# Six residual tiles with buffers of their own, and another model behind the scheduler's order

## The chip, the cores and the metric

The kernel runs on one core of a Trainium2 chip. The metric is device time in microseconds (us) of one execution. A profile is one execution taken by the hardware profiler; engines are named PE (TensorE, matrix products), PEld (its weight loads), DVE (VectorE), ACT (ScalarE), POOL (GpSimd) and SP (SyncE, here the queue that issues most DMAs).

## The reference, cut to what matters

Two networks in a row on a sequence of 512 positions with 1024 channels. The first has one block that mixes by a recurrence (8 heads) and by a stick-breaking attention (8 heads), joins both, and adds the result to its input. The second has two layers: a short convolution and a neighbourhood attention, each followed by a gated feed-forward, with a context of 256 positions beside it.

```
def first_block(x, c, ...):
    mod = silu(c) @ ada_w + ada_b              # shift, scale, gate
    h = rmsnorm(x, norm_g) * (1 + scale) + shift
    p = h @ w_in
    y_rwkv = rwkv7_group(p[..., :RWKV_COLS], ...)     # recurrence over 512 steps
    y_sb   = stick_breaking_group(p[..., RWKV_COLS:], sb_g)
    y = concatenate([y_rwkv, y_sb]) @ w_out
    x = x + gate * y                           # x is the residual
    return rmsnorm(x, final_g)

def second_block(x, c, ctx, c_ctx, ...):       # two layers
    for i in range(2):
        h, hc = modulate(rms_norm(x)), modulate(rms_norm(ctx))
        y, yc = conv_mixer(h), conv_mixer(hc)  # i == 0
        y     = neighbourhood_attention(h, hc) # i == 1
        x = x + g1 * y; x = x + g2 * swiglu(modulate(rms_norm(x)))
        # the context likewise, in layer 0 alone
    return x
```

## The kernel before

All activations stand transposed, as tiles of 128 channels x 512 positions (256 for the context). A product with full accuracy is made of three fp32r matmuls (`mm3`, L172 to L174): every weight and every activation is split into a high part (a cast on ACT, L155 for weights) and a low part (a subtraction on DVE, L156). Weights come from HBM on SP's queue in tiles `st` (L167, two buffers), and their split parts `wh`, `wl` have four buffers. Products are summed in two PSUM banks called `acc`.

Block 1 (`block1`) first normalises x and makes the modulation, then runs eight generators in turn: four recurrences `rwkv_pair` (two heads each, three steps to a pair) and four attentions `sb_pair`, in the fixed succession ORDER. A recurrence computes its inputs (L903: rm, km, vm), builds chunk matrices by many small matmuls (L978 to L1018), walks through eight chunks (L1056 to L1082) and normalises the outcome (L1085 to L1101). An attention computes, for each of four query blocks and two heads, scores (L1146), two Sigmoids (L1150, L1151), a scan and a product (L1155, L1157), transposes (L1161) with a copy (L1163), and values (L1168); then it normalises (L1171 to L1179). Meanwhile POOL loads and DVE reduces the modulations of later layers (L200, L210), at low priority.

The end of block 1 is the part `tail`. It is traced behind the last attention, `sb_pair(3)`, in a memory pool of that name, which lies where the recurrences' pool `rk` was. It holds:

- the context: eight loads of `xc` (L404), squares and their sum (L254 to L263), `rstd`, and the modulated `hc` (L287 to L290);
- the products with w_out in two parts. The first part needs six of the eight results (`yh`, in the succession YORD); the second the results of recurrence 3 and attention 3 (h3, h7). For m = 0 to 5 the first part is a product in `acc` (18 matmuls), a load of the residual tile `xt` (L418, one tag, two buffers), and L420, which computes part = acc x gate + xt and so frees the bank. For m = 6, 7 the first part stays in the two `acc` banks. The second part (from L443 on) completes all eight, adds the part (L450), and sums the squares for the next norm (L453 to L460). The tiles 6 and 7 of x are loaded by L433, in another pool.

Layer 0 (`layer0`) and layer 1 (`layer1`) follow: convolution and feed-forward as long rows of products, and the neighbourhood attention (`na_pair`) with scores, softmax, transposes and values for eight pairs of heads.

What sets the order: the program is traced in one succession, which gives each instruction its priority. The framework's scheduler then plays the program on a model of the machine: an instruction whose inputs and buffers are ready in the model is handed to its engine, the one traced earliest first. The succession so found is written into each engine's queue and each DMA queue. On the chip every queue runs strictly in it, each instruction waiting on semaphores for what it needs. Pools are opened with `reuse_waits="tile"`: a tile waits only for the tiles whose memory it takes. Some edges are drawn by hand (`order`), to keep functions of one ACT table together.

Of the kernel before, what the change touches and what calls it, by code (L numbers as in the profile page):

```python
# [8 lines left out]
F32 = mybir.dt.float32  # L9
# [8 lines left out]
S = 512  # L18
SC = 256
# [65 lines left out]
class K:  # L85
# [223 lines left out]
    def block1(self):  # L309
        nc, tc, A = self.nc, self.tc, self.A  # L310
# [12 lines left out]
        with self.open(name="n1", bufs=2) as npool:  # L323
# [13 lines left out]
            rstd = npool.tile([128, S], F32, tag="nzc", name="rstd")  # L337
# [40 lines left out]
        with self.open(name="sb", bufs=1) as sb:  # L378
            with self.open(name="rk", bufs=1) as rk:
                self.rk, self.sb = rk, sb  # L380
                pl = pre[12]
                zl = rk.tile([128, S], F32, name="zl")
                self.mix(pl, self.V("mu", 12), omu[:, 12:13], zl)
                nc.scalar.activation(zl[0:64], zl[0:64], AF.Tanh)
                self.y = y
                runs = [self.rwkv_pair(p, W, h, zl, omu, oka, pre) for p in range(4)]
                for n in ORDER[:-1]:
                    if n < 4:
                        next(runs[n], None)
                    else:  # L390
                        y[n] = self.sb_pair(n - 4, W, h, sb)
            self.xp = self.pool("xp", side="right")
            self.cxp = self.pool("cxp", side="right")
            self.hcp = self.pool("hc", side="right")
            self.xas = ExitStack()
            xa = self.xas.enter_context(self.open(name="xa", bufs=1, side="right"))
            y[7] = self.sb_pair(3, W, h, sb)
            if self.dbg:
                for k in range(8):
                    nc.sync.dma_start(A['dbg_y'][k], y[k])  # L400
            with self.open(name="tail", bufs=2) as tp:
                xc = self.xc = [self.cxp.tile([128, SC], F32, tag=f"xc{k}", name=f"xc{k}") for k in range(KT)]
                for k in range(KT):
                    nc.sync.dma_start(xc[k], A["ctx"][k])  # L404
                hc = self.hc = [self.hl(self.hcp, SC, f"hc{k}") for k in range(KT)]
                gc = self.gain("gc0", "norm_mix0", mod, 8, 1)
                pc = self.psum("py")[:, :SC]
                self.sumsq(xc, SC, tp, "c", pc)
                rstd = tp.tile([128, SC], F32, name="rstd")
                since = self.rsqrt(rstd, pc, since=self.sbexp)  # L410
                self.modulate(xc, range(KT), gc, mod, 0, 1, hc, tp, "cz", rstd)
                yh, part = [], []
                for k in YORD:
                    if k == 3:
                        for m in range(6):
                            po = self.xgemm(A["w_out"][m], yh, 0, 6)
                            xt = tp.tile([128, S], F32, tag="xt", name="xt")
                            nc.sync.dma_start(xt, A["x"][m // 2, :, m % 2])  # L418
                            t = self.yp.tile([128, S], F32, tag=f"y{YORD[m]}", name="part")
                            nc.vector.scalar_tensor_tensor(t, po, self.m1[:, 16 + m, 0:1], xt,  # L420
                                                           op0=ALU.mult, op1=ALU.add)
                            part.append(t)
                        for m in (6, 7):
                            po = self.psum("acc")
                            self.gemm(po, A["w_out"][m], yh, 0, 6, last=False)
                            part.append(po)
                        w2 = self.load_w(A["w_out2"][0], 1024) + self.load_w(A["w_out2"][1], 1024)
                    t = self.hl(self.hp, S, f"h{k}")
                    self.split(t, y[k])
                    yh.append(t)  # L430
# [13 lines left out]
        for n, m in enumerate((6, 7, 0, 1, 2, 3, 4, 5)):  # L444
            po, base = (part[m], xs[m]) if m >= 6 else (self.psum("acc"), part[m])
# [828 lines left out]
```

## Time and profile before

| | us |
|---|---|
| median of 3 runs (lowest to highest) | 2109.79 (2105.21 to 2114.11) |
| the profiled execution's own time | 2113.01 |
| its span, first to last instruction | 2111.2 |
| block 1: first product of layer 0 starts at | 545.4 |
| layer 1's attention, about | 1450 to 1740 |

The profile gives busy time by engine and views of the same execution: stretches (busy time of each engine between two moments), the timeline of one engine (start, duration, line, operation, and in brackets the idle time before it with what ended it), the waits (who waited for whom), the chain of work that ended last, and all instructions that touch a tile. Ends of matmuls are modelled, so a busy PE is not PE at its peak. The granted clock is given as a share of full speed. The lines stand in the prediction, where they are used.

### The profile page before, as it was taken

To read this page: it belongs to the slowest core of one execution; us is meant where nothing else is said; L and a number is where in the kernel's file an instruction comes from. 1 tells how busy PE (TensorE), PEld (TensorE's weight loads), DVE (VectorE), ACT (ScalarE), POOL (GpSimd) and SP (SyncE) were. 2 spreads that over 40 slices of the span, in tenths; PEclk is the share of its full clock that TensorE was granted. 3 is DMA by queue.
4 is the path that set the end of the run, shared out by engine and by line. 5 is a ranking of instruction groups with operands and counts; after the bars stand their busy time and mean duration, and the time that the engine had idled before them with its cause. 6 is when DMAs were issued, how large, how long until landed. Compare 5 with 4: busy or idle time off the path is not lost.

```text
span 2111.2 us, 33545 instructions
## 1 busy us (share of the span) xinstructions
PE 2055.6 (97%) x13596; PEld 1655.4 (78%) x13596; DVE 1233.2 (58%) x2641; ACT 796.4 (38%) x1485; POOL 131.4 (6%) x212
## 2 busy tenths in 40 slices
PE   6899999998999999999999999999999999999999
PEld 3676666665788888888888888898777787888887
DVE  3868887645777756767355443354566655434443
ACT  3436444345422224221122122244777744323232
POOL 0000000000000000001001000000233200000000
PEclk9999999987999999999999999999999999999999
DMA  7432312112233321435234322222111112333333
GB/s 285 139 101 82 112 59 86 55 52 74 70 127 128 125 80 50 150 120 180 88 122 154 115 91 58 63 81 70 43 59 61 36 63 90 99 100 93 97 99 101
DMA packets 61356, 203.60 MB, mean 96 GB/s; under 512 B 6928, under 2 KB 8976, under 8 KB 61200
## 3 DMA queue, kind: packets, MB, share of 16 engines
q1 hardware_dynamic: 45360, 145.77, 21.2%
q0 software_dynamic: 15120, 55.06, 8.1%
q8 instruction: 107, 1.75, 0.3%
q10 hardware_dynamic: 720, 0.62, 0.1%
q14 instruction: 49, 0.40, 0.1%
HBM read 199.32 MB, written 2.10 MB: 95 GB/s over the span
## 4 chain that ended last, share of the span: by engine, by line
PE 87%; ACT 3%; DVE 2%; issue 1%; POOL 0%; POOLq 0%; ACTq 0%; DVEq 0%
PE acc L173 20%; PE acc L172 19%; PE acc L174 19%; PE cacc L174 5%; PE cacc L173 5%; PE cacc L172 5%; PE py L894 2%; PE pT L874 2%; PE ss L1146 1%; PE so L1168 1%; PE sm L861 1%; PE sm L862 1%; PE py L1082 1%; PE py L1080 1%; PE ss L1161 1%
## 5 line engine op out<-in xcount | busy, mean ns | idle before, releaser
L155 ACT CAST wh<-st 128x512 fp32r<-128x512 f32 (+2 forms) x481 | 292.6, 609 | 733.4 <-PE acc L173 291.8
L156 DVE TENSOR_TENSOR wl<-st,wh 128x512 fp32r<-128x512 f32 (+2 forms) x481 | 324.1, 676 | 358.3 <-ACT wh L155 354.9
L172 PE MATMUL acc<-xzzh,wh 128*128 128x512 f32 x352 | 138.7, 394 | 0.0
L174 PE MATMUL acc<-xzzh,wl 128*128 128x512 f32 x352 | 138.0, 392 | 0.0
L173 PE MATMUL acc<-xzzl,wh 128*128 128x512 f32 x352 | 138.0, 392 | 0.0
L210 DVE CUSTOM_DVE_ANT_0 junk<-ast,cb,vec 128x512 bf16<-128x512 f32 x168 | 125.2, 745 | 18.2 <-DMA ast<-in_w_ada_dram 14.6
L210 DVE CUSTOM_DVE_ANT_0 junk<-ast,cb,m 128x512 bf16<-128x512 f32 x168 | 125.4, 747 | 2.8
L200 POOL DMA_DIRECT2D ast<-in_w_ada_dram x96 | 50.9, 530 | 1026.0 <-DVE m L210 954.6
L174 PEld LDWEIGHTS acc<-xzzh,wl 128*128 128x128 f32 x352 | 66.0, 188 | 14.9
L173 PEld LDWEIGHTS acc<-xzzl,wh 128*128 128x128 f32 x352 | 66.1, 188 | 13.5 <-issue 0.5
L172 PEld LDWEIGHTS acc<-xzzh,wh 128*128 128x128 f32 x352 | 66.1, 188 | 13.4 <-issue 0.5
L172 PE MATMUL acc<-h0h,wh 128*128 128x512 f32 (+1 forms) x164 | 65.9, 402 | 3.0 <-DVE fs L642 3.0
L173 PE MATMUL cacc<-czzl,wh 128*128 128x256 f32 x240 | 68.1, 284 | 0.0
L172 PE MATMUL cacc<-czzh,wh 128*128 128x256 f32 x240 | 67.7, 282 | 0.0
L174 PE MATMUL cacc<-czzh,wl 128*128 128x256 f32 x240 | 67.2, 280 | 0.0
L174 PE MATMUL acc<-h2h,wl 128*128 128x512 f32 (+1 forms) x164 | 65.8, 401 | 0.0
L173 PE MATMUL acc<-h3l,wh 128*128 128x512 f32 (+1 forms) x164 | 65.3, 398 | 0.3 <-DVE h3l L290 0.3
L173 PE MATMUL acc<-h1l,wh 128*128 128x512 f32 (+1 forms) x164 | 65.5, 399 | 0.0
L173 PE MATMUL acc<-h6l,wh 128*128 128x512 f32 (+1 forms) x164 | 65.4, 399 | 0.1
L173 PE MATMUL acc<-h5l,wh 128*128 128x512 f32 (+1 forms) x164 | 65.2, 398 | 0.0
L174 PE MATMUL acc<-h4h,wl 128*128 128x512 f32 (+1 forms) x164 | 65.2, 398 | 0.0
L174 PE MATMUL acc<-h0h,wl 128*128 128x512 f32 (+1 forms) x164 | 65.1, 397 | 0.0
(731 smaller groups left out, 5584.5 us busy)
## 6 DMA issues: line engine op xcount, KB each, us to landing
ast<-in_w_ada_dram POOLq DMA_DIRECT2D x96, 512.0 KB, 3.8
st<-in_ffn_w_in_dram SPq DMA_DIRECT2D x88, 512.0 KB, 3.5
st<-in_ffn_w_out_dram SPq DMA_DIRECT2D x32, 448.0 KB, 3.4
st<-in_w_in_dram SPq DMA_DIRECT2D x24, 512.0 KB, 3.5
st<-in_conv_w_in_dram SPq DMA_DIRECT2D x24, 512.0 KB, 3.5
ast<-in_ada_n_dram SPq DMA_DIRECT2D x16, 512.0 KB, 9.0
st<-in_ffn_w_out_dram SPq DMA_DIRECT2D x16, 512.0 KB, 3.5
st<-in_w_qk_dram SPq DMA_DIRECT2D x16, 512.0 KB, 3.5
```

Source lines behind the costliest of these rows:

```text
L155: nc.scalar.copy(hi[:, :n], sl)
L156: nc.vector.tensor_tensor(lo[:, :n], sl, hi[:, :n].bitcast(F32), ALU.subtract)
L172: mm(out, lhsT=lh, rhs=rh, start=first, stop=False)
L173: mm(out, lhsT=lh, rhs=rl, start=False, stop=False)
L174: return mm(out, lhsT=ll, rhs=rh, start=False, stop=last)
L200: self.nc.gpsimd.dma_start(st, src)
L210: i = self.nc.vector.tensor_tensor_reduce(out=junk, in0=st[:, hs], in1=c[:, hs], scale=0.5, scalar=o if hf else self.V(bname, j), op0=ALU. ...
L861: mm(o, lhsT=qh[:, e, qs], rhs=ks, start=True, stop=False)
L862: mm(o, lhsT=ql[:, e, qs], rhs=ks, start=False, stop=True)
L874: nc.tensor.transpose(pT[:, to], s[:, 128 * i:128 * i + 128], self.C("ident"))
L894: self.nc.tensor.matmul(po[r, cs], lhsT=v[:, r], rhs=pts[e][:, blk:blk + n].rearrange("p a t -> p (a t)"), start=i == 0, stop=i == len(wor ...
L1080: mm(o, lhsT=SV[e][:, c], rhs=MMt[e][:, c], start=True, stop=c == 0)
```

## The change

The six residual tiles get a buffer each and are allocated first in the tail's pool; their six loads are traced ahead of the context's, and L420 reads them. The tile `rstd` has one buffer in place of two. The scheduler is told by `schedule_with_timeline_sim=True` to play the program on another model, a timeline simulator, in place of the default one. That flag holds for the whole program, so the order in every queue of every block is made anew. Instructions, shapes and data stay the same.

```diff
             with self.open(name="tail", bufs=2) as tp:
+                xts = [tp.tile([128, S], F32, name=f"xt{m}", bufs=1) for m in range(6)]
+                for m in range(6):
+                    nc.sync.dma_start(xts[m], A["x"][m // 2, :, m % 2])
                 xc = self.xc = [self.cxp.tile([128, SC], F32, tag=f"xc{k}", name=f"xc{k}") for k in range(KT)]
...
-                rstd = tp.tile([128, SC], F32, name="rstd")
+                rstd = tp.tile([128, SC], F32, name="rstd", bufs=1)
...
                             po = self.xgemm(A["w_out"][m], yh, 0, 6)
-                            xt = tp.tile([128, S], F32, tag="xt", name="xt")
-                            nc.sync.dma_start(xt, A["x"][m // 2, :, m % 2])
                             t = self.yp.tile([128, S], F32, tag=f"y{YORD[m]}", name="part")
-                            nc.vector.scalar_tensor_tensor(t, po, self.m1[:, 16 + m, 0:1], xt,
+                            nc.vector.scalar_tensor_tensor(t, po, self.m1[:, 16 + m, 0:1], xts[m],
                                                            op0=ALU.mult, op1=ALU.add)
...
-    with tile.TileContext(nc) as tc, ExitStack() as ctx:
+    with tile.TileContext(nc, schedule_with_timeline_sim=True) as tc, ExitStack() as ctx:
         K(ctx, tc, A).build()
```

## The prediction

> **What bounds the kernel now.** I read the page first, then the table of stretches, then the end of block 1 queue by queue. The page gives the span, each engine's busy time, and the span in forty slices.
>
> ```profile
> span 2111.2 us, 33545 instructions
> PE 2055.6 (97%) x13596; PEld 1655.4 (78%) x13596; DVE 1233.2 (58%) x2641; ACT 796.4 (38%) x1485; POOL 131.4 (6%) x212
> PE   6899999998999999999999999999999999999999
> PEclk9999999987999999999999999999999999999999
> ```
>
> TensorE is busy 97% of the span, so little seems to be left. The slices show one dent: the granted clock falls to 7 tenths in the tenth slice, near 500 us. The table of stretches (its columns are the stretch, then the busy time and count of PE, PEld, DVE, ACT and POOL, the granted clock, the DMA share and GB/s) separates the regimes.
>
> ```profile
> 50.00:450.00 400.00, 388.08 (x4487) 268.58 (x4485) 307.77 (x737) 185.12 (x361) 16.21 (x31) 0.98 0.28 87
> 150.00:200.00 50.00, 49.36 (x258) 30.80 (x257) 42.46 (x101) 31.34 (x50) 2.12 (x4) 1.00 0.24 76
> 350.00:400.00 50.00, 49.97 (x496) 38.10 (x496) 36.95 (x89) 16.79 (x36) 1.59 (x3) 1.00 0.27 83
> 457.00:502.00 45.00, 33.99 (x129) 16.90 (x129) 19.43 (x42) 18.00 (x34) 0.00 (x0) 0.55 0.22 67
> 600.00:700.00 100.00, 100.00 (x572) 87.70 (x571) 71.13 (x176) 26.56 (x48) 6.36 (x12) 1.00 0.38 123
> 1450.00:1740.00 290.00, 284.05 (x1676) 221.07 (x1675) 177.05 (x398) 192.19 (x384) 62.85 (x78) 0.99 0.17 54
> ```
>
> At 600:700, as in most of what follows, PE runs one matmul behind the other: 100% busy, weight loads 88%. Another order can hardly make that faster. From 50 to 450 us PE also reads 97%, but weight loads fill only 268.58/400 = 67%, and DVE is at 77%: four recurrences and four attention pairs take turns, and their order decides. Layer 1's attention (1450:1740) lies between: 76%. From 457 to 502 us PE is busy 34.0 of 45 us at clock 0.55, the one plain hole in the kernel.
>
> Why the hole is there is seen in three queues. First PE:
>
> ```profile
> 456.82 0.40 PE L174 MATMUL acc<-h6h,wl 128*128 128x512 f32 x1
> 502.17 0.62 PE L172 MATMUL acc<-h0h,wh 128*128 128x512 f32 x1
> 509.07 0.39 PE L172 MATMUL acc<-h0h,wh 128*128 128x512 f32 x1
> 529.27 0.39 PE L174 MATMUL acc<-h6h,wl 128*128 128x512 f32 x1
> 529.49 0.39 PE L172 MATMUL acc<-h3h,wh 128*128 128x512 f32 x1
> ```
>
> Two of the eight first-part w_out products (18 matmuls each) are finished by 457.2 us; the third starts at 502.17, and the eighth ends where the second part (h3, h7) starts, at 529.49. In between PE has only the last attention pair, the last recurrence's end and the context's sums. Then DVE, and SP with the two longest waits of its queue there:
>
> ```profile
> 496.82 0.94 DVE L258 TENSOR_TENSOR acc<-acc,sq 128x256 f32<-128x256 f32 x2
> 497.69 1.40 DVE L420 SCALAR_TENSOR_TENSOR part<-acc,m,xt 128x512 f32<-128x512 f32 x2
> ...
> 469.69 3.66 SPq L404 DMA_DIRECT2D xc<-in_ctx_dram  x8
> 473.40 0.90 SPq L418 DMA_DIRECT2D xt<-in_x_dram  x2
> 474.40 13.53 SPq L433 DMA_DIRECT2D x<-in_x_dram  x2
> 498.46 11.95 SPq L418 DMA_DIRECT2D xt<-in_x_dram  x3
> ...
> SPq L433 <- DVE BK L1099: 12.7, 1, 12.7
> SPq L404 <- PE sc L1058: 11.4, 1, 11.4
> ```
>
> The two products wait in both acc banks of PSUM for L420, which runs at 497.69, behind the context's squares on DVE. L420 needs xt. On SP's queue xt stands behind the context's loads (L404, which waited 11.4 us for a buffer of the recurrence), and the third xt stands behind L433 and behind L420 itself, since xt has two buffers. So a late residual tile holds two banks, and the banks hold PE.
>
> **The change, part by part.** *Six buffers.* It adds no transfer: the six loads of L418 stay, are issued first in the tail, and their waits for L420 go. Six tiles of 2 KB at the start of the tail's pool lie where the recurrence had zl, t3, rm, km and the two buffers of vm, in order of first use (2, 2, 2, 2, 2.5 and 2.5 KB), so the first five come free when pair 3 has read km and rm, and the sixth when it has read vm:
>
> ```profile
> L957 DVE TENSOR_TENSOR XY<-km,t x8: 674/683/689, 77.0 to 347.7; 64x512 f32<-64x512 f32 x8
> L960 DVE TENSOR_TENSOR RA<-rm,PP x4: 680/682/693, 80.7 to 352.8; 128x512 f32<-128x512 f32 x4
> L1098 DVE TENSOR_TENSOR tb<-vm,rsm x4: 679/682/686, 176.1 to 483.9; 128x512 f32<-128x512 f32 x4
> L1101 DVE TENSOR_TENSOR y<-BK,gs x4: 682/687/692, 181.5 to 487.6; 128x512 f32<-128x512 f32 x4
> 376.23 1.06 PE rsm L1097 x2
> 492.87 0.43 ACT L254 ACTIVATE acc<-xc 128x256 f32<-128x256 f32 x1
> DMA to landing us min/median/max: 2.6/2.7/4.1
> ```
>
> Five tiles can be there at about 381 us (pair 2's last read of vm follows the product of L1097 at 376.23, the third of four; then 2.7 us to land), 90 us earlier than now; the sixth at 484.6 + 2.7 = 487. Its product is the sixth in line, so it is hardly waited for. The single rstd buffer costs nothing: rstd is written once. But the context's acc, squares and rstd move up by 12 KB, to where pair 3 has vm and gs: a new wait, until L1101 ends at 488.3. The squares run at 492.87 today, so 4.6 us cover it; planned earlier, they would hold ACT's queue, and the pair's sigmoids behind them, until 488.
>
> *What then fills the hole.* With xt there, L420 can follow each product at once (0.75 us), and six more products of 18 matmuls can run from 457 on. In the undisturbed run from 509.07 to 529.49, 90 matmuls took 20.42 us, 0.227 us each, so six products are 108 x 0.227 = 24.5 us. The hole's own PE work, 33.99 us at clock 0.55, is 18.7 us at full clock (one form in it shows the ratio):
>
> ```profile
> 473.93 2.08 PE L1087 MATMUL rsm<-BK,con 128*128 128x512 f32 x2 [0.27 <-ACT BK L1085]
> 371.82 0.89 PE rsm L1087 x2
> ```
>
> 18.7 + 24.5 = 43.2 us of 45: it just fits, and PE is then so full that the attention pair's chain gains at most 2 us from the clock. What is late next is h7, the split of that pair's output:
>
> ```profile
> 511.36 1.09 DVE L1179 TENSOR_TENSOR y<-ors,sgs 128x512 f32<-128x512 f32 x1
> 512.48 0.62 ACT L306 CAST h7h<-y 128x512 fp32r<-128x512 f32 x1
> 523.09 0.69 DVE L307 TENSOR_TENSOR h7l<-y,h7h 128x512 fp32r<-128x512 f32 x1
> ```
>
> Now h7l is made at 523.09 because nothing hurries; it could be at 513.1 + 0.7 = 513.8. The second part then starts at 513.8 in place of 529.49: 15.7 us. With the 2 us of the chain I take 18 us. The bounds are 0 (the hole stays) and 27.3 us (all from 502.17 to 529.49). What hides the context's modulate (DVE, 511 to 522 us) is today the first part; it would lie beside the second part (11.5 us), and is due only at the first context product after it.
>
> *The order of everything.* Nothing in the trace shows what order the other model gives. The program is the same; each queue's order may differ everywhere. At 600:700 and its like I take nothing: PE is full there. In layer 1's attention PE idles 290 - 284 = 6 us, and the best density would give 290 - 221/0.877 = 38; by its own PE row I take nothing there either and leave the rest to a rival. For 50 to 450 us I bound it by the best and worst of its eight 50 us stretches: at the density of weight loads of 350:400 (38.10/50) the 268.58 us of loads would take 352 us, 48 less; at that of 150:200 (30.80/50) 436 us, 36 more. I take the middle of these two, 6 us less, since no row is nearer to one end.
>
> Sum against the profiled execution (span 2111.2, its own time 2113.0): 2113.0 - 18 - 6 = 2089. The median shown is 2109.8, 3.2 lower, so I forecast 2086 us.
>
> The Trainium skill ("Perfetto Trace Analysis", section Identifying the Most-Contended Engine) says that matmul occupancy is no measure of the distance from the limit and that the weight loads' share should be read. By PE's own row at 50:450 an order could give back only 400 - 388 = 12 us, by the page's measure a multiple of it, and the forecast would be the same. The rows side with the page: two stretches that both read 97% or more have weight loads of 67% and 88%.
>
> **Rivals.** *More than the tail* (0.18): the new order is better for the intertwined stages; up to 48 us in block 1 and 18 in the tail is 2044; half of that gain, 24 and 18, is 2068. Layer 1's attention could add to it. For it: no engine is at its limit there. Against: the queues are in order, and a plan helps only where its durations are the chip's.
>
> *The hole stays or half of it* (0.17): SP is one queue, and both L433 and L404 stood at its head for 12 us while later loads could have gone. If x (L433) or the sixth xt, free only at 484 us, is planned ahead of the remaining w_out weights, those products wait for weights until 487. Then 12.7 of the 18 us are lost, and with no gain elsewhere it is 2110 - 5 = 2105. This includes the case that the flag hardly alters the order.
>
> *Slower* (0.23): the scalar engine's function tables. The score blocks use Sigmoid, the recurrence and the norms Ln and Exp, and each alternation loads a table:
>
> ```profile
> 172.77 1.28 ACT L236 ACT_TABLE_LOAD   x1
> 174.08 0.69 ACT L242 ACTIVATE Z<-rsm,epsb 128x512 f32<-128x512 f32 x1
> 174.79 1.28 ACT L1151 ACT_TABLE_LOAD   x1
> 176.09 0.49 ACT L1151 ACTIVATE om<-ss 128x384 f32<-128x384 f32 x1
> 176.59 1.28 ACT L248 ACT_TABLE_LOAD   x1
> ```
>
> Here one Sigmoid fell between an Ln and its Exp: three loads in 5.1 us, in the middle of a chain. The hand-made edges of the program pin only some pairs, and the timeline model, by its source, prices no table load. There are 32 score blocks; if each gets one load more, that is 32 x 1.283 = 41 us on ACT, and where ACT ends the chain (score, sigmoid, scan) it is paid in full: 2086 + 41 = 2127. It decides from 24/1.283 = 19 extra loads on. Against it: ACT is busy 185 of 400 us, so part of them would be covered.
>
> By the Trainium skill ("ScalarE: Activation LUTs", section What ACT_TABLE_LOAD costs) a switch costs about 2.66 us, load and drain together; then nine extra loads would decide. The rows disagree: the load at 174.79 begins 0.02 us after the Ln ends and the Sigmoid 0.02 us after the load, so 1.28 us is what I use.
>
> **How the numbers follow.** The forecast has 0.42 with a range of its own of 2066 to 2100; the others 0.18, 0.17 and 0.23. A measurement of this kernel tells some 0.5%, 10.5 us, from no change: faster is below 2099.2, slower above 2120.3. Faster: 0.42 + 0.18 = 0.60; within: 0.17; slower: 0.23. Range: low 2045 (nearly the full 48 us and the tail; 0.07 below it), high 2135 (the worst density, 36 us, with half of the tail's gain lost would be 2137; 0.12 above).
>
> **What would show it.** In the profile after: xt landing before 400 us for five of six; L420 within some 2 us of each product; no stretch near 480 us with a clock below 0.9; w_out's second part starting about 16 us earlier relative to the last attention pair's end; the 600:700 regime the same. Wrong if L420 still runs behind the context's squares, if SP holds weights behind L433, if the table loads of block 1 grow by twenty, or if PE shows new idle after 600 us.

## The result: slower, 2279 us

| | before | after |
|---|---|---|
| median of the runs, us | 2110.66 (4 runs, 2105.21 to 2114.11) | 2279.12 (4 runs, 2277.14 to 2280.94) |
| ratio to before | | 1.0800, 95% interval 1.0785 to 1.0815 |
| block 1, to the first product of layer 0's context | 545.4 | 672.2 |
| layer 0's convolution, to the first Tanh of its feed-forward | 291.0 | 292.7 |
| that feed-forward, to layer 1's first values | 561.5 | 568.0 |
| values, to the attention's first transpose | 77.3 | 87.5 |
| the attention, first to last transpose | 219.0 | 239.2 |
| from there to layer 1's first Tanh | 59.4 | 60.6 |
| the rest | 357.6 | 356.6 |

The lower rows are differences of start times in the two traces. Of the 165.6 us between the spans, 126.8 are lost in block 1 and 30.4 in layer 1's attention with its values. The long rows of products lose little. The forecast was 2086 us, so even the sign was wrong.

The page of the changed kernel: span, each engine's busy time, and PE and its clock in forty slices.

```profile
span 2276.8 us, 33634 instructions
PE 2130.7 (94%) x13596; PEld 1720.5 (76%) x13596; DVE 1238.0 (54%) x2641; ACT 805.8 (35%) x1493; POOL 130.4 (6%) x212
PE   7998887988699999999999999999998989999999
PEclk9996675966599999999999999999999999999999
```

The number of matmuls is the same. The clock, which had one dent before, is now at 5 to 7 tenths in seven of the first eleven slices, and PE has gaps in most of them. The table of stretches (stretch, then busy time and count of PE, PEld, DVE, ACT and POOL, the clock, the DMA share and GB/s) says it in numbers:

```profile
50.00:450.00 400.00, 355.77 (x3418) 257.03 (x3416) 264.06 (x621) 161.36 (x285) 17.06 (x32) 0.79 0.26 86
150.00:200.00 50.00, 41.83 (x401) 28.92 (x401) 47.50 (x118) 21.29 (x45) 4.22 (x8) 0.65 0.36 117
550.00:600.00 50.00, 36.45 (x541) 24.51 (x537) 16.19 (x38) 13.19 (x31) 0.00 (x0) 0.57 0.01 2
700.00:800.00 100.00, 100.00 (x573) 87.80 (x572) 70.64 (x179) 26.13 (x49) 6.34 (x12) 1.00 0.38 122
```

The last row is the full regime, which reads as before (100.00, 87.70). The first is the stretch that I had bounded: in 400 us, 3418 matmuls now and 4487 before. From 150 to 200 us DVE is near its limit (47.50 of 50 us); at 550 to 600 no engine is, and everything waits in turn. Why is seen when only one line of the products is counted. L172 is one third of the products with weights; the columns are those of PE and PEld, then clock, DMA share and GB/s. First the kernel before:

```profile
350.00:400.00 50.00, 17.63 (x50) 9.59 (x51) 1.00 0.27 83
400.00:450.00 50.00, 10.70 (x26) 4.57 (x26) 1.00 0.09 26
```

Then the changed kernel:

```profile
350.00:400.00 50.00, 3.48 (x7) 1.70 (x7) 0.56 0.00 1
400.00:450.00 50.00, 22.61 (x66) 12.26 (x65) 0.99 0.21 68
450.00:500.00 50.00, 5.33 (x12) 2.50 (x12) 0.60 0.03 9
...
550.00:600.00 50.00, 0.00 (x0) 0.00 (x0) 0.57 0.01 2
```

Before, the large products are spread over the recurrences and attentions and fill their waits. After, they come in heaps, and between heaps the chains run alone, at little more than half clock. In the traces' PE records from 40 us to the end of block 1, some 1055 such matmuls stand in 200 uninterrupted runs (median length 4) before, and in 51 runs (median 19, nearly a whole product of 24) after. In the attention of layer 1 it is 489 in 88 runs (median 2) before, 452 in 31 (median 19) after.

What a heap does to a chain is seen in the timeline of PE, in the triangular inverse of a recurrence. There L1002 and L1007 alternate, each with a short step of DVE (L1003, L1008) between them. The columns are start, duration, line and operation.

```profile
310.07 1.08 PE L1007 MATMUL pT<-Qc,XZ 32*32 32x32 f32 x64 [0.23 <-DVE Qc L1003]
311.63 0.79 PE L172 MATMUL acc<-h0h,wh 128*128 128x512 f32 x1 [0.48 <-DVE rm L904]
...
314.78 0.63 PE L173 MATMUL acc<-h2l,wh 128*128 128x512 f32 x1
...
315.56 0.39 PE L172 MATMUL acc<-h3h,wh 128*128 128x512 f32 x1
...
317.86 0.39 PE L173 MATMUL acc<-h6l,wh 128*128 128x512 f32 x1
318.18 0.75 PE L1002 MATMUL pQ<-XZ,Uc 32*32 32x32 f32 x64
...
323.84 0.75 PE L1007 MATMUL pT<-Qc,XZ 32*32 32x32 f32 x64
...
326.34 0.75 PE L1002 MATMUL pQ<-XZ,Uc 32*32 32x32 f32 x64
327.95 0.75 PE L1007 MATMUL pT<-Qc,XZ 32*32 32x32 f32 x64 [0.86 <-DVE Qc L1003]
329.22 0.75 PE L1002 MATMUL pQ<-XZ,Uc 32*32 32x32 f32 x64 [0.52 <-DVE XZ L1008]
```

DVE's part of the first step in the same execution:

```profile
311.49 0.41 DVE L1008 TENSOR_TENSOR XZ<-XZ,pT 128x256 f32<-128x256 f32 x1
311.93 0.45 DVE L1009 STREAM_TRANSPOSE XZ<-XZ 128x256 f32<-128x256 f32 x1
```

XZ is ready at 312.4; L1002, which needs it, runs at 318.18, because the 20 large matmuls from 311.63 to 317.86 stand ahead of it in PE's queue. Three steps, from 310.07 to 326.34, take 16.3 us; without heaps between them two steps, from 326.34 to 329.22, take 2.9. In the kernel before, the same steps have some four large matmuls between them and follow at 1.8 to 2.5 us:

```profile
215.01 0.75 PE L1006 MATMUL pT<-Qc,XZ 32*32 32x32 f32 x64
...
217.46 0.75 PE L1001 MATMUL pQ<-XZ,Uc 32*32 32x32 f32 x64
...
219.26 0.75 PE L1006 MATMUL pT<-Qc,XZ 32*32 32x32 f32 x64
...
221.07 0.75 PE L1001 MATMUL pQ<-XZ,Uc 32*32 32x32 f32 x64
```

The products of the heap are then behind, and the next steps have nothing beside them. The last walk is alone for another reason. Six of the eight first-part products with w_out are still to come, but nothing of L172 to L174 runs between these two, 83 us apart:

```profile
541.49 0.39 PE L174 MATMUL acc<-h6h,wl 128*128 128x512 f32 x1
624.88 0.80 PE L172 MATMUL acc<-h0h,wh 128*128 128x512 f32 x1 [4.33 <-DVE part L421]
```

They wait for L421, as in the hole before, and L421 now stands behind the y of an even later recurrence. So the hole that the tiles did not cure is probably part of the loss; the flag together with the tiles in another pool (see below) was not run.

A recurrence ends with y, four times in block 1; before, the first and the last were at 181.5 and 487.6:

```profile
L1102 DVE TENSOR_TENSOR y<-BK,gs x4: 679/686/691, 291.0 to 622.1; 128x512 f32<-128x512 f32 x4
```

Two more readings. L210, the low-priority reductions of later modulations, come earlier on DVE and make up half of its work from 100 to 200 us (stretches of L210 alone; the first two rows are before, the other two after):

```profile
100.00:200.00 100.00, 25.41 (x68) 0.97 0.30 96
300.00:400.00 100.00, 20.34 (x54) 0.98 0.27 84
```

```profile
100.00:200.00 100.00, 48.01 (x129) 0.79 0.40 128
300.00:400.00 100.00, 0.00 (x0) 0.66 0.07 22
```

And the residual tiles, of which five were to be there before 400 us: the instructions of L421, then SP's longest wait for them.

```profile
L421 DVE SCALAR_TENSOR_TENSOR part<-acc,m,xt x6: 737/742/751, 624.1 to 645.5; 128x512 f32<-128x512 f32 x6
```

```profile
SPq L404 <- DVE tb L1099: 76.0, 1, 76.0
```

The sixth load held SP's queue for 76.0 us, and L421 ran only behind pair 3's y. So both halves of the change have to be explained: what the flag did, and why the tiles did nothing.

### The profile page after: what moved, and what is told of

Same layout as the page of the kernel before. It is cut to its first block, busy times and chain, and to the rows that moved or that the text cites. A ratio compares the mean times of both kernels' runs of the same rounds, so it can differ in the third digit from the quotient of the medians.

```text
span 2276.8 us, 33634 instructions
## 1 busy us (share of the span) xinstructions
PE 2130.7 (94%) x13596; PEld 1720.5 (76%) x13596; DVE 1238.0 (54%) x2641; ACT 805.8 (35%) x1493; POOL 130.4 (6%) x212
## 4 chain that ended last, share of the span: by engine, by line
PE 80%; DVE 7%; issue 7%; ACT 5%; DMA 1%; POOL 0%; DVEq 0%; ACTq 0%; POOLq 0%
PE acc L172 18%; PE acc L173 18%; PE acc L174 18%; PE cacc L174 5%; PE cacc L173 5%; PE cacc L172 5%; PE py L895 1%; PE ss L1147 1%; PE pT L875 1%; DVE wl L156 1%; PE so L1169 1%; PE sm L862 1%; DVE pt L876 1%; DMA ast<-in_w_ada_dram 1%; DVE cum L1156 1%
## 5 line engine op out<-in xcount | busy, mean ns | idle before, releaser
L172 PE MATMUL acc<-xzzh,wh 128*128 128x512 f32 x352 | 138.4, 393 | 0.0
L174 PE MATMUL acc<-xzzh,wl 128*128 128x512 f32 x352 | 138.1, 392 | 0.0
L210 DVE CUSTOM_DVE_ANT_0 junk<-ast,cb,vec 128x512 bf16<-128x512 f32 x168 | 125.3, 746 | 21.5 <-DMA ast<-in_w_ada_dram 18.0
L210 DVE CUSTOM_DVE_ANT_0 junk<-ast,cb,m 128x512 bf16<-128x512 f32 x168 | 125.4, 747 | 2.4
L172 PE MATMUL acc<-h0h,wh 128*128 128x512 f32 (+1 forms) x164 | 69.8, 427 | 23.2 <-DVE k L820 12.3
L174 PEld LDWEIGHTS acc<-xzzh,wl 128*128 128x128 f32 x352 | 66.0, 188 | 14.7
L172 PEld LDWEIGHTS acc<-xzzh,wh 128*128 128x128 f32 x352 | 66.1, 188 | 13.3 <-issue 0.2
L173 PEld LDWEIGHTS acc<-xzzl,wh 128*128 128x128 f32 x352 | 66.1, 188 | 13.2 <-issue 0.2
L172 PE MATMUL cacc<-czzh,wh 128*128 128x256 f32 x240 | 68.0, 283 | 0.0
L174 PE MATMUL acc<-h0h,wl 128*128 128x512 f32 (+1 forms) x164 | 67.0, 409 | 0.9 <-DVE wl L156 0.9
L174 PE MATMUL cacc<-czzh,wl 128*128 128x256 f32 x240 | 67.8, 283 | 0.0
L173 PE MATMUL acc<-h0l,wh 128*128 128x512 f32 (+1 forms) x164 | 67.1, 410 | 0.7 <-DVE h0l L290 0.7
L173 PE MATMUL acc<-h2l,wh 128*128 128x512 f32 (+1 forms) x164 | 66.6, 407 | 0.0
L174 PE MATMUL acc<-h1h,wl 128*128 128x512 f32 (+1 forms) x164 | 66.3, 405 | 0.0
L172 PE MATMUL acc<-h1h,wh 128*128 128x512 f32 (+1 forms) x164 | 66.1, 405 | 0.0
L172 PE MATMUL acc<-h2h,wh 128*128 128x512 f32 (+1 forms) x164 | 65.6, 405 | 0.5 <-ACT h2h L306 0.5
```

The costliest lines, as they stand in the source:

```text
L172: mm(out, lhsT=lh, rhs=rh, start=first, stop=False)
L173: mm(out, lhsT=lh, rhs=rl, start=False, stop=False)
L174: return mm(out, lhsT=ll, rhs=rh, start=False, stop=last)
L210: i = self.nc.vector.tensor_tensor_reduce(out=junk, in0=st[:, hs], in1=c[:, hs], scale=0.5, scalar=o if hf else self.V(bname, j), op0=ALU. ...
```

## The experiments

Eleven runs. "Block 1" is again the time to the first product of layer 0's context, in the profiled execution. Each run was timed against the kernel before on the same chip; those medians were 2107.84 to 2110.5 us.

### The two halves apart

The six tiles alone are the change without the last hunk of the diff; the flag alone is this:

```diff
-    with tile.TileContext(nc) as tc, ExitStack() as ctx:
+    with tile.TileContext(nc, schedule_with_timeline_sim=True) as tc, ExitStack() as ctx:
```

> The six residual tiles alone, scheduled by the default model. Theory H (the tiles at SP's head): SP issues the six residual loads ahead of the context's, the sixth waits for pair 3's last reading of vm and everything behind it on SP waits too; the first w_out products' L420 still comes only after pair 3's end, so nothing of the hole is filled. Time 2100 to 2125 (0 to +12 against before, about 2111). Rival P (my prediction's step): five tiles lie there early, six more products fill the hole, second part 16 us earlier: 2093, at least 10 below before.

> The flag alone, with before's residual tiles (one tag, two buffers). If the whole loss is the order's: within 10 us of the changed kernel, 2270 to 2290. If the six tiles' load at SP's head (76.0 us of waiting in the changed kernel's trace) is a loss of its own: 2200 to 2250, 30 us or more faster than the changed kernel. If the two need each other: near 2111.

The tiles alone: 2107.66 us, ratio 0.9989 (0.9968 to 1.0011), block 1 548.9. The flag alone: 2279.41, ratio 1.0792 (1.0747 to 1.0837), block 1 677.2. So the whole loss is the flag's, and the 76.0 us for which SP's queue stood still in the changed kernel cost nothing that can be measured.

The first run also shows which step of my prediction on the tiles fell. Four views of it: the instructions on the tile xt, SP's waits, the ends of the two products that wait (their last matmul is that of h6), and DVE's timeline.

```profile
L404 SPq DMA_DIRECT2D xt<-in_x_dram x6: 328/433/1603, 462.0 to 487.5; - x6
L421 DVE SCALAR_TENSOR_TENSOR part<-acc,m,xt x6: 724/742/752, 496.6 to 525.4; 128x512 f32<-128x512 f32 x6
DMA to landing us min/median/max: 2.9/4.0/4.5
```

```profile
SPq L404 <- DVE tb L1099: 22.0, 1, 22.0
```

```profile
L174 PE MATMUL acc<-h6h,wl x2: 397/397/397, 448.8 to 460.5; 128*128 128x512 f32 x2
```

```profile
490.60 0.69 DVE L1102 TENSOR_TENSOR y<-BK,gs 128x512 f32<-128x512 f32 x1
495.49 1.22 DVE L1156 TENSOR_TENSOR_SCAN cum<-om,one 128x512 f32<-128x512 f32 x1 [4.20 <-ACT om L1152]
496.63 0.72 DVE L421 SCALAR_TENSOR_TENSOR part<-acc,m,xt 128x512 f32<-128x512 f32 x1
```

The first load goes out at 462.0 and lands some 4 us later. Both products are finished by then (448.8 and 460.5). L421 still runs at 496.63, because that is its place in DVE's queue: behind pair 3's y and the next scan. The first tile was there 30 us early, and the plan, it seems, had not counted on it. In the queues of the kernel before, of this run and of the changed kernel alike, no such part stands ahead of pair 3's y, the last use of the recurrences' pool beneath the tail's.

### The residual tiles in another pool

To test that, the tiles were put where the plan has memory earlier: into the buffers `ast` of the modulations' pool, which stays open, as three tiles of two.

```diff
-                            xt = tp.tile([128, S], F32, tag="xt", name="xt")
-                            nc.sync.dma_start(xt, A["x"][m // 2, :, m % 2])
+                            if m % 2 == 0:
+                                xt2 = self.ap.tile([128, D], F32, tag="ast", name="xt2", bufs=2)
+                                nc.sync.dma_start(xt2, A["x"][m // 2].rearrange("p a n -> p (a n)"))
+                            xt = xt2[:, S * (m % 2):S * (m % 2) + S]
```

> Before's default model, the residual tiles as three double tiles in the modulation's weight buffers, which are free long before the tail and lie in a pool that stays open. If the hole at 457 to 502 us is held by the residual tiles alone, as my prediction has it, the first-part products run in it and the time falls by 12 to 20 us, to 2091 to 2099. If what holds the hole is something else (the attention's chain at a low clock, the second part's own inputs), 2106 to 2114.

2088.3 us (2086.76 to 2091.47), ratio 0.9885 (0.9846 to 0.9925), just below the range that I had given; block 1 524.3, 21.1 less than before. It is the fastest kernel of this study, without the flag. The parts and who waited for them, and the stretch of the old hole:

```profile
L422 DVE SCALAR_TENSOR_TENSOR part<-acc,m,xt x6: 743/750/753, 444.5 to 497.6; 128x512 f32<-128x512 f32 x6
...
  POOL ast L200: 155.9, 2
```

```profile
457.00:502.00 45.00, 44.55 (x236) 28.87 (x236) 31.16 (x65) 24.39 (x49) 1.59 (x3) 1.00 0.37 117
```

The parts now run from 444.5, beside recurrence and attention 3, the stretch that had 129 matmuls at clock 0.55 has 236 at 1.00, and PE is busy 44.55 of 45 us. The modulations' loads on POOL wait 155.9 us for their buffers; the time after block 1 is not longer for it (1565.4 us, before 1565.7). The run agrees with the reading that the plan hands out the tail's memory late; the rule by which it does so is not shown.

### Which queue carries the flag's loss in block 1

In the next runs the flag is on, the tiles are before's, and the succession of single queues in block 1 is held to that of the kernel before, by edges without semaphores between neighbours of a list (the lists are left out):

```diff
+def pin(tc, nc, orders):
+    at = {i.name: i for i in nc.cur_bb.bb.instructions}
...
+            if last is not None:
+                tc.add_manual_dep(i, last, dep, reason="queue order")
+            last = i.name
...
-        K(ctx, tc, A).build()
+        k = K(ctx, tc, A)
+        k.build()
+        pin(tc, nc, (PE_ORDER,))
```

The expectations for TensorE alone, VectorE alone, both, and all five queues:

> The flag with before's residual tiles, and TensorE's queue through block 1 held to the succession that it has in the kernel before; all other queues, and all of TensorE's after block 1, as the timeline model orders them. Theory T-PE (whole w_in products stand in TensorE's queue ahead of the chains' steps, then the chains run alone): block 1 comes back to 545 to 565 us from 672, and the time to 2140 to 2165. Rival T-DVE (low-priority reductions and other work on DVE and ACT ahead of the chains): block 1 stays above 620 us, the time above 2220.

> The flag, with VectorE's queue alone held through block 1 to the succession of the kernel before. With TensorE's queue held alone, block 1 fell from 677.2 to 603.2 us, so 57.8 of its 131.8 us of loss lie elsewhere. Theory A (two separate losses, TensorE's 74 and VectorE's early reductions about 58, which add up): block 1 at 615 to 625 us, time 2215 to 2230. Theory B (TensorE's bunched queue is enough by itself to hold the chains, so VectorE alone gives little): block 1 above 650, time above 2250. Theory C (VectorE's queue is the root): block 1 below 600, time below 2200.

> The flag, with TensorE's and VectorE's queues held through block 1 to before's succession. If the reductions on VectorE are what was left with TensorE's queue held: block 1 at 545 to 560 us, time 2145 to 2165. If it is ScalarE's queue (its eight more table loads, about 10 us, or the splits of weights in another succession): block 1 at 580 or above, time 2180 or above.

> The flag, with all five queues held through block 1 to before's succession (instructions of later blocks may still stand between them). All theories: block 1 within 5 us of 545.4; the time is then before's plus what the flag costs after block 1, 35.7 us by the traces (2278.7 - 677.2 against 2111.2 - 545.4): 2140 to 2152. A time at 2111 would say that the later loss only follows from block 1's.

And the other way round, the flag's queue of TensorE in the kernel before, with edges made from the flag's succession and the default model for everything else:

> The other way round: the kernel before, default model, with TensorE's queue alone held through block 1 to the succession that the timeline model gave it; the other queues are planned around it. If the bunched queue is enough by itself (as the run with VectorE's queue alone held says, block 1 at 690): block 1 at 640 to 700, time 2205 to 2265, and nothing lost after block 1. If it needs the flag's VectorE queue beside it: block 1 below 620, time below 2185.

| queues of block 1 held to before's | block 1, us | median, us | ratio (interval) |
|---|---|---|---|
| none (the flag alone) | 677.2 | 2279.41 | 1.0792 (1.0747 to 1.0837) |
| VectorE | 690.4 | 2294.45 | 1.0887 (1.0871 to 1.0904) |
| TensorE | 603.2 | 2202.96 | 1.0417 (1.0367 to 1.0467) |
| TensorE and VectorE | 551.6 | 2161.76 | 1.0261 (1.0234 to 1.0287) |
| all five | 545.4 | 2155.46 | 1.0227 (1.0209 to 1.0244) |
| no flag, TensorE's queue as the flag has it | 673.6 | 2241.34 | 1.0614 (1.0591 to 1.0638) |
| no flag: the kernel before | 545.4 | 2107.84 to 2110.5 | |

Block 1 is read from the one profiled execution of each kernel, and that of the run with TensorE held was the slowest of its four (2209.06); so differences between these rows are sure to a few us only. My two numbers for TensorE alone (below 565, above 620) were both missed: 603.2 lies between. With all five queues held, block 1 came out as expected, the time 3.5 us above its range. TensorE's succession is enough by itself: with it, the default model's other queues give 673.6, and VectorE's old succession gives nothing (690.4; with it held, the new plan still has TensorE's products in heaps, 68 runs of median length 14). The bounded stretch in the kernel before with the flag's TensorE queue:

```profile
50.00:450.00 400.00, 345.95 (x3416) 250.32 (x3415) 266.10 (x624) 155.07 (x282) 17.06 (x32) 0.79 0.24 85
```

That is nearly the changed kernel's row (3418 matmuls, clock 0.79). The edges fix TensorE's whole succession, though, the chains' steps as well as the large products, and the chains' turns differ too: before, the last recurrence ends 24 us ahead of the last attention (488.3 and 512.5), in the changed kernel 47 us behind it (622.8 and 575.4). No run varied the heaps alone, so that they are the cause within this queue rests on the timelines above. Without the flag's succession on TensorE a second loss appears, VectorE's: 603.2 - 551.6 = 51.6 us (41.2 by the medians). The two do not add up as separate terms: 74.0 for TensorE alone, -13.2 for VectorE alone, 125.6 for both, of 131.8. ScalarE, SP and POOL together hold the last 6.2, no more than two executions of one kernel may differ (the first four of the kernel before lie 8.9 apart).

### What on VectorE

With TensorE's queue held, VectorE's list was split: first without the 96 reductions of L210 that belong to block 1, then with the reductions and only the instructions just ahead of them.

> The flag, through block 1 TensorE's queue held, and VectorE's too except for the modulations' reductions (L210), which go where the timeline model puts them: the median one behind 183 of block 1's other 683 VectorE instructions, against 251 in the kernel before and 111 with TensorE's queue alone held. If early reductions are VectorE's loss (51.6 us between the runs with TensorE held and with both held, 603.2 and 551.6): half of the way, block 1 at 570 to 590, pair 0's y 10 to 25 us later than 186. If it is the succession of the chains' own VectorE work: block 1 at 550 to 556.

> The complement: TensorE's queue held, and on VectorE only the reductions held behind the instruction that they follow in the kernel before; the rest of VectorE's queue as the timeline model orders it, apart from what that leaves no choice. If early reductions are VectorE's loss: block 1 at 550 to 562, time 2150 to 2170. If the chains' own succession is: block 1 at 590 to 605, time near 2200.

Reductions free: block 1 577.4, 2185.95 us, ratio 1.0345 (1.0317 to 1.0374). Reductions held, the rest free: 586.7, 2192.07 us, ratio 1.038 (1.0352 to 1.0407). Neither theory alone: the reductions' early places cost 577.4 - 551.6 = 25.8 us where everything else is held (24.2 by the medians). Holding them alone gives back 603.2 - 586.7 = 16.5, but 10.9 by the medians, and there the intervals of the two ratios overlap, so this second figure is not clear of noise. The other part, the succession of the chains' own VectorE work, was not taken further apart.

### Layer 1's attention

> As the run before it, and TensorE's queue in layer 1's attention held too. If the attention's loss (some 20 us in its span, 10 us ahead of it) is TensorE's queue again: 20 to 30 us less than the run before it, 2115 to 2130. If it lies in VectorE's or ScalarE's queue or in the loads there: within 8 us of it.

2128.21 us, ratio 1.0119 (1.0084 to 1.0154), against 2155.46: 27 us back, as the first theory had it. The stretches of the attention, before, with block 1 alone held, and with TensorE's queue in the attention held too:

```profile
1475.00:1695.00 220.00, 214.38 (x1300) 162.44 (x1298) 140.42 (x333) 157.94 (x322) 62.34 (x78) 0.98 0.16 50
```

```profile
1495.00:1735.00 240.00, 213.78 (x1259) 163.84 (x1257) 140.82 (x333) 155.26 (x318) 61.56 (x77) 0.96 0.14 44
```

```profile
1485.00:1708.00 223.00, 210.79 (x1292) 161.60 (x1293) 140.55 (x329) 157.48 (x319) 61.36 (x78) 0.99 0.15 49
```

The same work of every engine in 220, 240 and 223 us. What is left over the kernel before (20 us by the medians, 13 by the traces) lies in small pieces: by the traces 5.4 us in layer 0's feed-forward and 3 to 4 each in the values and the attention. These were not tried.

## Why the prediction was wrong, step by step

**The bound.** Right in its regimes: the full one is the same to 0.1% after, and the intertwined ones are where order decides. All of the large loss is in those.

**The hole and its cause.** Right: the banks held for L420 held PE. With the parts early, the stretch is full (44.55 us of PE where I had worked out 43.2) and block 1 is 21.1 us shorter; I had taken 18, for a change that puts the tiles where they can be had. That the two are near is in part luck, for the split was wrong. In the run with the other pool the last attention and the second part stand so:

```profile
500.16 1.09 DVE L1181 TENSOR_TENSOR y<-ors,sgs 128x512 f32<-128x512 f32 x1
505.62 0.39 PE L172 MATMUL acc<-h3h,wh 128*128 128x512 f32 x1
```

The attention's y starts 11.2 us earlier than before (511.36), in a stretch at clock 1.00 in place of 0.55; I had allowed the chain 2 us. The second part follows that start by 5.5 us in place of 18.1: 12.7 us, where I had taken 15.7. A reading was off as well: the row 371.82 0.89, set beside 473.93 2.08 for the clock's ratio, is from the chain that ended last; the timeline has 1.05 us there.

**"Five tiles can be there at about 381 us".** Failed. I followed when the memory comes free on the chip; the queues fit a plan that has it later, and a queue follows the plan. With the tiles alone the loads went out from 462.0, the tile stood ready 30 us, and L421 kept its place behind pair 3's y. The gain of this half cannot be told from 0 (ratio 0.9989, 0.9968 to 1.0011), my own lower bound. "The sixth tile is hardly waited for" also failed as a statement on SP (22.0 us alone, 76.0 with the flag), but it cost nothing that can be measured. The same holds of the single rstd buffer and the context's move over pair 3's memory.

**"The order of everything", -48 to +36 us, taken as -6.** This is the step that made the prediction wrong: it was +131.8 in block 1 (the flag alone) and, at nothing taken, some 30 in layer 1's attention with its values. The bound came from the densest and the thinnest 50 us stretch of the kernel before. But both are stretches of a plan that lays the products among the chains. A new order can undo that, and then no stretch of the old trace is a bound. After, whole stretches have weight loads of 24.51 of 50 us, below the 30.80 that I had called the worst. A better estimate could have been had from the trace before: some 1055 matmuls of 0.227 us are 240 us of filling work, and an order that sets all of it apart from the chains would lose about that. It is no bound either, since chains alone also ran at a lower clock. About half of it was lost.

**The rivals.** "More than the tail" did not occur: block 1 and the attention both became longer. "The hole stays" is what the tiles alone did, and SP did stand behind the sixth of them, but what kept the hole was L421's place on DVE. "Slower" ended on the right side by the wrong mechanism. ScalarE has 8 more loads of tables than before (1493 instructions against 1485), some 10 us at 1.283 each, fewer than the 19 from which it was to decide. That the timeline model prices no table load is shown by no run here. And the kernel before with the flag's TensorE queue has only 3 more and loses 128.2 us in block 1:

```profile
PE 2110.6 (94%) x13596; PEld 1704.3 (76%) x13596; DVE 1237.0 (55%) x2641; ACT 802.1 (36%) x1488; POOL 131.2 (6%) x212
```

**What would show it.** Five tiles before 400 us: no. L420 close behind its product: no, neither in the changed kernel nor with the tiles alone. A clock below 0.9: seven slices. The second part 16 us earlier behind the last attention: not in the changed kernel, 12.7 us with the tiles in the other pool. The full regime unchanged: yes.

What stays open is why the timeline model takes whole products ahead of the chains. The runs show what its order costs, and that it does so with VectorE's succession held too; nothing here shows which of the model's durations or rules makes it.

## What to carry to other kernels

A switch that makes every queue anew is not bounded by the old trace's best and worst stretch. Count the filling work that the old order lays between dependent steps; if a new order heaps it, a large part of it can come on top (here about half), and the number to look at is how many large matmuls stand in a row between two steps of a chain. And an earlier buffer is worth something only if the plan sees it earlier: look whether the reader's place in its queue moved, not only whether the tile landed.

## What the runs showed of the hardware

The changed order costs twice. Where PE waits between chain steps its granted clock is lower, and the chain's own matmuls take longer. By the two pages the 165.6 us are 90.5 more of idle PE and 75.1 more of busy PE for the same number of matmuls (2130.7 against 2055.6; their ends are modelled). In the recurrences' walk four matmuls `sc` took 0.34 us in the kernel before, among large products, and 0.48 in the changed kernel, alone:

```profile
439.86 0.34 PE L1058 MATMUL sc<-VS,AL 128*64 128x64 f32 x4
```

```profile
589.74 0.48 PE L1059 MATMUL sc<-VS,AL 128*64 128x64 f32 x4
590.55 0.48 PE L1064 MATMUL sc<-Rh,Z 64*64 64x64 f32 x4 [0.33 <-DVE Rh L1061]
```

Gaps of a third of a microsecond between such steps (PE's longest wait there is 2.5 us) go with a clock of 0.57 for the whole stretch from 550 to 600. The way back is seen in one place: in the timeline of the inverse above, the large matmuls take 0.63 us until 314.78 and 0.39 from 315.56 on, 3.9 us after the first of the heap.
